# A depthwise convolution of 31 taps as three filters of half the taps, in a kernel ordered by a planner

## The chip, the cores and the metric

The kernel runs on one core of a Trainium2 chip. The metric is device time of one launch in microseconds (us). Before the change the median of three runs is 1378.37 us (1372.61 to 1379.06).

The engines are named as in the profile: PE (TensorE, matmuls; PEld its weight loads), DVE (VectorE), ACT (ScalarE), POOL (GpSimd) and SP (SyncE, which here only issues transfers). SBUF is the memory on the core, PSUM the small memory that PE writes its results to.

## The reference

One inference step of a streaming encoder of two layers, on 512 frames of a new stream ("prompt") and 64 frames of a running one ("sample"), with 1024 channels, all in fp32. A layer, cut to what matters:

```python
p = x @ w_in                                  # [q | k | v | conv_a | conv_gate]
q, k, v, ca, cg = split(p)
attn = differential_attention(rope(q), rope(k), v)      # 4 heads, two softmaxes each
u = ca * sigmoid(cg)                          # 512 channels
full = concat([hist, u], axis=1)              # 30 older frames ahead of the new ones
c = conv(full, conv_w) + conv_b               # each channel by itself, causal, 31 taps
c = silu(layer_norm(c))
y = concat([attn, c]) @ w_out
x = layer_norm(DEEPNORM_ALPHA * x + y)
h = square(relu(x @ w_ff1))                   # 4096 wide
x = layer_norm(DEEPNORM_ALPHA * x + h @ w_ff2)
```

The outputs are x of both streams, and the new keys, values and last 30 convolution inputs of each layer.

## The kernel before

**Data.** x is kept transposed: eight tiles of 128 channels by 576 frames, 512 of the prompt and 64 of the sample. Most work is done in two halves of 288 frames. `r` tiles hold the running fp32 values, `x` and `a` tiles the split operands of matmuls.

**Matmuls.** An fp32 product is made of three matmuls of a reduced fp32 type (`tri`, L734 to L736): high part of the weight by high part of x, high by low, low by high. A weight unit is 128 x 1024. It is loaded into `raw` by SP's queue, and ACT makes the high part `wh` (L891). The low part `wl` is made in one of two ways. Either DVE or POOL subtracts the high part from `raw` (L894). Or, "by transfer": ACT writes minus the high part into `wl` (L875), POOL issues a transfer that adds the weight from memory into it (L878), and ACT writes `wh` (L881). A number `DM` for each stage says what share of the units goes by transfer. While layer 0's FFN runs, 20 weight units of layer 1 are split in advance and stored (`split_ahead`). The FFN's products are taken in pairs with shared sums and differences (L2162, L2030, L1884, L2056, L2273).

**Stages of a layer.** Mixing (input projection, attention, convolution), then the output projection with the first LayerNorm, the FFN, and the FFN's last part with the second LayerNorm. In the attention, the softmax of a block of queries runs over DVE (the maximum, L1486; reciprocals, L1517; the difference of the two softmaxes, L1530) and ACT (the exponential, L1502), and PE transposes the result (L1539). L1615 and L1625 scale its output.

**The convolution** (`conv`, L1305). The 512 channels are four tiles. For each, `ub` holds 30 older frames, 512 of the prompt, 30 older, and 64 of the sample: 636 in a row, and the 606 results (UC) include 30 that nobody needs. `NPTS[t]` of the 31 taps are made by ACT (a product, L1322) and POOL (a sum, L1325), 9 to 12 a tile, into an `r` tile. The others are made by DVE, one instruction a tap (L1337: frames times the tap plus what is there), accumulating in a PSUM tile `sc` read as 2 x 303. Three sums (`fin`, L1344) add the two. Behind it, the channels are added up over tiles (L1669), PE makes the mean (L1679), a reciprocal root is found by a short chain of DVE steps on 96 x 6 values (`rstd`, L959 to L987), and the result is split into high and low parts for the output projection (L1761 and the line behind it).

**The LayerNorms.** The attention's and the convolution's parts of the output projection come in turn. The first is added to alpha x in two steps (L1799, and L1804 for the other summand), the second by L1857. The channel tiles are summed (L1835) and PE makes the mean from that; L1052 subtracts it, L1058 and L1064 square and add up, L1133 multiplies by the reciprocal root, L1141 scales and shifts on ACT, and L1154 makes the low part.

**What sets the order.** Each step is a node with a cost for each engine that may do it (`cV`, `cA`, `cG`, `cP`, `cD` for DVE, ACT, POOL, PE and the load queue), a latency, buffers that it takes and gives back, and a priority. `Sched.run` goes through time with these costs and gives each engine, when it is free in the plan, the ready node of highest priority. In that order the instructions are then issued: nothing is reordered on the chip, an engine runs its rows one after the other. Eight tables of numbers (`PHASES`, one for each of four stages in each layer) set priorities, the share by transfer, the order of weight units and who takes which step. The semaphore waits between instructions follow from which tiles they read and write.

## Time and profile before

| | |
|---|---|
| median of three runs | 1378.37 us (1372.61, 1379.06, 1378.37) |
| the profiled execution's own time | 1375.67 us |
| its span, first to last instruction | 1373.9 us, 24858 instructions |
| mean granted clock of TensorE | 0.977 |
| PE, DVE, ACT, POOL busy | 1308.0, 1078.1, 705.1, 302.3 us |
| transfers | 186.38 MB, mean 136 GB/s |

The stages stand at about 18 to 290 us (mixing and first LayerNorm of layer 0), 290 to 671 (its FFN), 671 to 700 (second LayerNorm), 700 to 965, 965 to 1349 and from 1349 (the same of layer 1). Busy times are sums over the whole span; a stage's own limit is read from its own window. A chain of waits is followed back from the last instruction, and names for each stretch the engine that was then being waited for.

### The profile page before, as it was taken

What the parts mean: (1) busy time and instruction counts of PE and PEld (TensorE: products, weight loads), DVE (VectorE), ACT (ScalarE), POOL (GpSimd) and SP (SyncE); (2) the same over time, 40 slices, a digit from 0 to 9 for tenths busy, and PEclk for the clock granted to TensorE, in tenths of its full rate; (3) what the DMA queues carried; (4) which work ended last, traced back from release to release, by engine and by line L of the source; (5) the groups of instructions that cost most, each with busy time, mean ns of one, the idle gap of its engine ahead of it and who ended that gap; (6) DMA issues with size and microseconds to landing.
All of it is one profiled execution on the core that took longest, in us unless ns stands there. A gap on an engine that the chain in (4) does not pass through costs nothing.

```text
span 1373.9 us, 24858 instructions
## 1 busy us (share of the span) xinstructions
PE 1308.0 (95%) x9518; PEld 1264.1 (92%) x9518; DVE 1078.1 (78%) x2206; ACT 705.1 (51%) x1413; POOL 302.3 (22%) x292
## 2 busy tenths in 40 slices
PE   8989989979999999999999999899989999999997
PEld 7878879979899999999998988798889999999996
DVE  5899998777888887878658999868677676767737
ACT  5766677265444444434156657754654443434424
POOL 0456620150000000000144885223400000000013
PEclk9999989989999999999999999899999999999998
DMA  6635533334465645554345444454234343435262
GB/s 220 162 94 140 122 117 106 93 130 156 144 211 165 208 168 192 185 167 139 102 158 204 160 152 121 129 135 118 64 79 117 112 108 108 124 80 144 70 152 69
DMA packets 70102, 186.38 MB, mean 136 GB/s; under 512 B 10848, under 2 KB 16608, under 8 KB 69984
## 3 DMA queue, kind: packets, MB, share of 16 engines
q1 hardware_dynamic: 63504, 161.20, 34.9%
q0 software_dynamic: 6480, 23.60, 10.4%
q8 instruction: 75, 1.23, 0.4%
q14 instruction: 43, 0.35, 0.1%
HBM read 154.11 MB, written 30.65 MB: 134 GB/s over the span
## 4 chain that ended last, share of the span: by engine, by line
PE 72%; DVE 18%; issue 3%; DMA 2%; ACT 2%; POOL 2%; SPq 0%; ACTq 0%; DVEq 0%; POOLq 0%
PE b L734 21%; PE b L735 21%; PE b L736 21%; DVE sc L1337 8%; DMA raw<-in_wu_dram 2%; PE sc L734 1%; PE b L1006 1%; POOL sq L1064 1%; PE sc L736 1%; PE b L1568 1%; PE sc L735 1%; DVE nm L1486 1%; DVE P L1530 1%; DMA wl<-in_wu_dram 1%; PE b L1611 1%
## 5 line engine op out<-in xcount | busy, mean ns | idle before, releaser
L734 PE MATMUL b<-x,wh 128*128 128x288 f32 x1356 | 416.2, 307 | 6.6 <-ACT wh L891 4.0
L736 PE MATMUL b<-x,wl 128*128 128x288 f32 x1356 | 406.1, 299 | 7.0 <-DVE wl L894 4.8
L735 PE MATMUL b<-x,wh 128*128 128x288 f32 x1356 | 406.5, 300 | 1.7 <-DVE x L1215 1.1
L734 PE MATMUL b<-a,wh 128*128 128x288 f32 x1088 | 325.0, 299 | 0.2 <-ACT x L731 0.2
L735 PE MATMUL b<-a,wh 128*128 128x288 f32 x1088 | 321.3, 295 | 0.0
L736 PE MATMUL b<-a,wl 128*128 128x288 f32 x1088 | 321.0, 295 | 0.0
L734 PEld LDWEIGHTS b<-x,wh 128*128 128x128 f32 x1356 | 260.5, 192 | 13.5 <-ACT wh L891 4.0
L736 PEld LDWEIGHTS b<-x,wl 128*128 128x128 f32 x1356 | 260.2, 192 | 8.2 <-DVE wl L894 5.3
L735 PEld LDWEIGHTS b<-x,wh 128*128 128x128 f32 x1356 | 260.6, 192 | 4.0 <-DVE x L1215 2.5
L734 PEld LDWEIGHTS b<-a,wh 128*128 128x128 f32 x1088 | 205.1, 188 | 2.0 <-issue 0.6
L735 PEld LDWEIGHTS b<-a,wh 128*128 128x128 f32 x1088 | 205.4, 189 | 0.5
L736 PEld LDWEIGHTS b<-a,wl 128*128 128x128 f32 x1088 | 205.1, 188 | 0.0
L2273 DVE TENSOR_TENSOR r<-r,b 128x288 f32<-128x288 f32 x192 | 85.7, 450 | 87.6 <-PE b L736 87.3
L1337 DVE SCALAR_TENSOR_TENSOR sc<-ub,par,sc 128x606 f32<-128x606 f32 x160 | 136.2, 851 | 4.2
L878 POOL DMA_DIRECT2D wl<-in_wu_dram x45 | 39.2, 871 | 446.8 <-ACT wl L875 387.6
L1064 POOL TENSOR_TENSOR sq<-sq,sq 128x288 f32<-128x288 f32 x40 | 35.7, 910 | 416.1 <-ACT sq L1058 415.5
L1325 POOL TENSOR_TENSOR r<-r,prod 128x606 f32<-128x606 f32 x72 | 113.7, 1580 | 54.8 <-ACT prod L1322 31.0
L891 ACT CAST wh<-raw 128x1024 fp32r<-128x1024 f32 (+1 forms) x73 | 71.4, 979 | 71.2 <-PE b L735 52.3
L2056 ACT CAST wh<-ckv 128x512 fp32r<-128x512 f32 x104 | 64.1, 620 | 76.7 <-PE b L735 61.2
L894 DVE TENSOR_TENSOR wl<-raw,wh 128x1024 fp32r<-128x1024 f32 (+1 forms) x73 | 84.5, 1161 | 22.3 <-ACT wh L891 21.7
L1884 DVE TENSOR_TENSOR wl<-ckv,wh 128x512 fp32r<-128x512 f32 x104 | 71.1, 685 | 6.0 <-ACT wh L2056 5.8
L875 ACT ACTIVATE wl<-raw 128x1024 fp32r<-128x1024 f32 x45 | 47.7, 1060 | 44.2 <-PE b L736 25.5
(320 smaller groups left out, 2409.9 us busy)
## 6 DMA issues: line engine op xcount, KB each, us to landing
raw<-in_wu_dram SPq DMA_DIRECT2D x110, 512.0 KB, 4.6
wl<-in_wu_dram POOLq DMA_DIRECT2D x45, 512.0 KB, 7.2
wscr<-cs SPq DMA_DIRECT2D x80, 256.0 KB, 2.0
ckv<-in_wu_dram SPq DMA_DIRECT2D x26, 512.0 KB, 3.6
ah<-in_wu_dram SPq DMA_DIRECT2D x26, 512.0 KB, 4.4
cs<-in_wu_dram SPq DMA_DIRECT2D x40, 256.0 KB, 2.8
wh<-wscr SPq DMA_DIRECT2D x20, 512.0 KB, 3.3
wl<-wscr SPq DMA_DIRECT2D x20, 512.0 KB, 4.4
```

The source lines that it names most:

```text
L734: TE.matmul(o, wh, xh, start=start, stop=False)
L735: TE.matmul(o, wh, xl, start=False, stop=False)
L736: TE.matmul(o, wl, xh, start=False, stop=stop)
L875: S.activation(wt["lo"], wt["raw"], AF.Copy, scale=-1.0)
L891: S.copy(wt["hi"][:, c], wt["raw"][:, c])
L894: e.tensor_tensor(wt["lo"][:, c], wt["raw"][:, c], wt["hi"][:, c].bitcast(F32), op=ALU.subtract)
L1064: e.tensor_tensor(q[a]["t"], q[a]["t"], q[b]["t"], op=ALU.add)
L1325: GP.tensor_tensor(cc[t], cc[t], st[j], op=ALU.add)
L1337: V.scalar_tensor_tensor(st["a0"], win(j), w, st["a0"], op0=ALU.mult, op1=ALU.add)
L1884: e.tensor_tensor(o, a, b, op=ALU.subtract)
L2056: S.copy(tl["wh"][box["i"]][:, off:off + n], src())
L2273: V.tensor_tensor(rr, rr, bk(), op=ALU.add)
```

## The change

**The convolution in three filters.** Call the even frames e, the odd ones o, and the 31 taps' even and odd numbered ones w0 and w1 (16 and 15). One kind of output needs w0 on e plus w1 on o, the other w0 on o plus w1 on e. The change makes three filters of half the frames: a = w0 on e (16 taps), b = w1 on o (15 taps, with the bias), and c = the sums of neighbouring taps on s = e + o (16 taps). The second kind of output is then c minus a minus b. So 47 taps of 303 frames take the place of 31 taps of 606. e and o are read from `ub` with a step of two frames; s lies unit by unit.

- b is made on ACT and POOL (304 frames wide, the first `NPTS[t]` taps, at most 15), and any further taps by DVE.
- s is one sum on DVE or POOL (318 frames).
- a (L1414) and c (L1421) are made on DVE by turns, a tap of one, then a tap of the other. Both accumulate in one PSUM tile `sc`, a in its first half, c in its second.
- `fin` has six instructions (256 and 32 frames, for a + b, c - b, and that minus a). The result lies with its even frames first, and is put back in turn where it is split into high and low parts (`halves`).
- `params` makes the summed taps `cv` once a layer.

```diff
         def conv(t, start, outs):
-            npt = NPTS[t]
+            npt = min(NPTS[t], W // 2)
...
+            def frames(odd, i, n):
+                return ub[t].rearrange("p (n two) -> p two n", two=2)[:, odd, i:i + n]
...
-                a = op({"A": cA(UC, 1 if j else 2)}, pa, (*start, pd), acq=("r",) if j == 0 else ("prod",), pri=PT)
+                a = op({"A": 0.46 if j else 0.5}, pa, (*start, pd), acq=("r",) if j == 0 else ("prod",), pri=PT)
...
+            def both(e):
+                e.tensor_tensor(cc[t][:, :UH], frames(0, 0, UH), frames(1, 0, UH), op=ALU.add)
+            sm = op({"V": cV(UH), "G": cG(UH)}, both, (*start, cc["n", t]), pri=PT)
             vt = None
-            for j in range(npt, W):
+            for j in range(W // 2 + 1):
                 def va(e, j=j):
...
-                        V.scalar_tensor_tensor(st["a0"], win(j), w, st["a0"], op0=ALU.mult, op1=ALU.add)
-                vt = op({"V": cV(UC, True) + 0.06}, va, (*start, pd, vt), acq=("cv", "sc") if j == npt else (), pri=PT)
+                    if j == 0:
+                        st["s"] = take("sc")
+                        st["a"], st["c"] = st["s"][:, 0, :YH], st["s"][:, 1, :YH]
...
+                        V.scalar_tensor_tensor(st["a"], frames(0, j, YH), w, st["a"], op0=ALU.mult, op1=ALU.add)
+                def vc(e, j=j):
...
+                        V.scalar_tensor_tensor(st["c"], cc[t][:, j:j + YH], w, st["c"], op0=ALU.mult, op1=ALU.add)
+                vt = a_end = op({"V": 0.45}, va, (*start, pd, vt), acq=("cv", "sc") if j == 0 else (), pri=PT)
+                vt = op({"V": 0.45}, vc, (sm, vt, ld_n), pri=PT)
...
             def fin(e):
-                for o, i, b, c, n in ((0, 0, 0, 0, hc), (hc, hc, 1, 0, SEQ - hc), (SEQ, S0, 1, S0 - hc, DEC)):
-                    V.tensor_tensor(a1[:, o:o + n], a1[:, i:i + n], a0[:, b, c:c + n], op=ALU.add)
+                parts = ((0, 0, SEQ // 2), (SEQ // 2, S0 // 2, DEC // 2))
+                for o, i, n in parts:
+                    V.tensor_tensor(cc[t][:, o:o + n], st["a"][:, i:i + n], b_(n, i), op=ALU.add)
+                for o, i, n in parts:
+                    V.scalar_tensor_tensor(cc[t][:, T // 2 + o:T // 2 + o + n], st["c"][:, i:i + n], cv[:, t, 0:1],
+                                           b_(n, i + 1), op0=ALU.add, op1=ALU.subtract)
+                for o, i, n in parts:
+                    z = cc[t][:, T // 2 + o:T // 2 + o + n]
+                    V.tensor_tensor(z, z, st["a"][:, i:i + n], op=ALU.subtract)
```

**The plan.** A low part by transfer had a fixed latency of 6.5 us in the plan. Now it has 1.9 + 2.93, plus what the load queue is still busy with, and 2.93 us are booked on that queue. Costs are changed too: a tap of a or c 0.45 us, `fin` 1.4 for 0.9, a step of the reciprocal root 0.16 for 0.075 and the root as one node 1.75 for 1.6, a load of x 200 for 144 columns, and the extra 0.1 (`PD`) that a PE node waited for another engine's result is gone. A filler matmul (`keep`, `spare`) is added with its share `FT` at 0, so that none is issued. All eight tables of `PHASES` are written anew.

```diff
-PD = 0.1
-DM, GD, GDL = 0.0, 0.88, 6.5
+PD = 0.0
+DM, GD, GDL, GDS = 0.0, 0.88, 1.9, 2.93
...
+                        if n.dm:
+                            n.lat = GDL + n.dm + max(0.0, busy["D"] - t - c)
+                            busy["D"] = max(busy["D"], t + c) + n.dm
...
-                los.append(op({"G": GD}, acc, (m,), lat=GDL, pri=pri + 1000, two=False))
+                los.append(op({"G": GD}, acc, (m,), lat=GDL + GDS, pri=pri + 1000, two=False))
+                los[-1].dm = GDS
...
-            m = op({"V": 0.075}, s, (m,), pri=pri, two=True)
+            m = op({"V": 0.16}, s, (m,), pri=pri, two=True)
...
-  'NPT': '9,10,12,12',
+  'NPT': '14,16,16,13',
```

**How the order moves.** In a row, the line comes first, then the operation, the tile written and those read with the numbers of their buffers, the shape, and the semaphores waited for: one for each engine or transfer queue whose work must have come so far.

DVE, layer 0, the first taps of the first channel tile, before (L1335, L1337), between rows of the attention's softmax:

```order
L1335 TENSOR_SCALAR sc_119<-ub_544,par_161 128x2x303 [waits DMAHW3_49,Pool_49]
L1517 RECIPROCAL rc_598<-sums_592 128x2 [waits Activation_49]
L1518 TENSOR_TENSOR rc_598<-rc_598,nlam_162 128x1 [waits DVE_49]
L1337 SCALAR_TENSOR_TENSOR sc_119<-ub_544,par_161,sc_119 128x2x303
L1337 SCALAR_TENSOR_TENSOR sc_119<-ub_544,par_161,sc_119 128x2x303 [waits DVE_49]
L1485 MEMSET sc_118 64x2x64 [waits PE_49]
L1486 TENSOR_REDUCE nm_596<-sc_118 128x2 [waits DVE_49]
L1337 SCALAR_TENSOR_TENSOR sc_119<-ub_544,par_161,sc_119 128x2x303
L1530 SCALAR_TENSOR_TENSOR P_603<-P_603,rc_598 128x128 [waits Activation_49]
L1337 SCALAR_TENSOR_TENSOR sc_119<-ub_544,par_161,sc_119 128x2x303 [waits DVE_49] x3
```

A tap waits for DVE's own count when the row ahead of it is the tap that it adds to.

DVE, layer 0, after the change, the first taps of the second tile (L1412 and L1414 are filter a, L1419 and L1421 filter c):

```order
L1412 TENSOR_SCALAR sc_118<-ub_881,par_161 128x303 [waits DMAHW4_49,DVE_49,Pool_49]
L1580 TENSOR_REDUCE nm_962<-sc_119 64x2
L1582 TENSOR_REDUCE nm_962<-b_114 64x1
L1582 TENSOR_REDUCE nm_962<-b_115 64x1
L1583 TENSOR_TENSOR nm_581<-nm_962 64x2 [waits DVE_49]
L1419 TENSOR_SCALAR sc_118<-r_93,par_161 128x303 [waits Pool_49]
L1414 SCALAR_TENSOR_TENSOR sc_118<-ub_881,par_161,sc_118 128x303 [waits DVE_49]
L1421 SCALAR_TENSOR_TENSOR sc_118<-r_93,cv_165,sc_118 128x303 [waits DVE_49]
```

The taps now come in pairs, one of each filter.

DVE, layer 0, a little later in the same tile, where rows of other work stand between two taps:

```order
L1036 SCALAR_TENSOR_TENSOR ary_1211<-art_1213,ary_1211 96x6
L1039 SCALAR_TENSOR_TENSOR ary_1211<-arh_1215,ary_1211 96x6 [waits DVE_49]
L1048 SCALAR_TENSOR_TENSOR dg_1237<-ident,ary_1211 96x576 [waits DMAHW7_49,DVE_49]
L1414 SCALAR_TENSOR_TENSOR sc_118<-ub_881,par_161,sc_118 128x303
L1421 SCALAR_TENSOR_TENSOR sc_118<-r_93,cv_165,sc_118 128x303 [waits DVE_49]
L1414 SCALAR_TENSOR_TENSOR sc_118<-ub_881,par_161,sc_118 128x303 [waits DVE_49]
L1706 SCALAR_TENSOR_TENSOR ob_853<-ob_853,gs_163,b_114 128x288 [waits PE_49,Activation_49]
```

The first tap behind other rows has no wait; those right behind a tap of the other filter have one, though they read and write the other half of the tile.

PE, layer 1, around the mean of the convolution's LayerNorm (L1679), before, with score matmuls of the attention ahead of it and the first matmuls of the next product behind:

```order
L736 MATMUL sc_118<-ckh_8234,a_8037 128x512
L734 MATMUL b_116<-a_8527,a_8036 128x64
L735 MATMUL b_116<-a_8528,a_8036 128x64
L736 MATMUL b_116<-a_8527,a_8037 128x64
L1679 MATMUL sc_119<-sgm_101,ones_h 128x288 [waits DVE_49]
L1679 MATMUL sc_119<-sgm_101,ones_h 128x288
L734 MATMUL b_115<-x_7307,wh_83 128x288 [waits DMAHW1_49]
```

Here the mean is the first thing behind the scores.

PE at the same place after the change (L1770; L781 to L783 are the three matmuls of `tri`, L1630 is the softmax's transpose):

```order
L783 MATMUL b_117<-x_7468,wl_87 128x288
L781 MATMUL b_117<-x_7472,wh_83 128x288
L782 MATMUL b_117<-x_7473,wh_83 128x288
L783 MATMUL b_117<-x_7472,wl_87 128x288
L1770 MATMUL sc_119<-sgm_101,ones_h 128x288 [waits DVE_49,Activation_49]
L1770 MATMUL sc_119<-sgm_101,ones_h 128x288
L1630 MATMUL b_115<-ident,P_9267 128x128 [waits DVE_49]
```

The mean now stands behind matmuls of a projection, 990 rows behind the end of layer 0's last LayerNorm where it was 925; in layer 0 it is PE's row 985 where it was 1017.

DVE, layer 0, before, where the output projection's second part is added (L1857) and the tiles are summed for the first LayerNorm's mean (L1835):

```order
L1835 TENSOR_TENSOR sg_107<-sg_107,r_98 128x288 [waits DVE_49]
L1857 TENSOR_TENSOR r_94<-r_94,b_116 128x288 [waits PE_49]
L1835 TENSOR_TENSOR sg_107<-sg_107,r_94 128x288 [waits DVE_49]
L1857 TENSOR_TENSOR r_92<-r_92,b_115 128x288 [waits PE_49]
L1835 TENSOR_TENSOR sg_107<-sg_107,r_92 128x288 [waits DVE_49]
L1857 TENSOR_TENSOR r_93<-r_93,b_114 128x288 [waits PE_49]
L1835 TENSOR_TENSOR sg_107<-sg_107,r_93 128x288 [waits DVE_49]
```

Each sum follows the addition that it needs, on the same engine.

POOL, after the change, the same sums (L1927), with the residual additions (L1896, before L1804) ahead of them:

```order
L1896 TENSOR_TENSOR r_98<-r_98,x_2467 128x288 [waits DMAHW6_49,DVE_49]
L1896 TENSOR_TENSOR r_94<-r_94,x_2492 128x288 [waits DMAHW7_49,DVE_49]
L1927 TENSOR_TENSOR sg_107<-r_97,r_91 128x288 [waits DVE_49]
L1927 TENSOR_TENSOR sg_107<-sg_107,r_95 128x288 [waits DVE_49,Pool_49]
L1927 TENSOR_TENSOR sg_107<-sg_107,r_92 128x288 [waits DVE_49,Pool_49]
L1927 TENSOR_TENSOR sg_107<-sg_107,r_96 128x288 [waits DVE_49,Pool_49]
L1927 TENSOR_TENSOR sg_107<-sg_107,r_93 128x288 [waits DVE_49,Pool_49]
```

The sums for this mean, a chain in which each waits for the one ahead, have moved from DVE to POOL, and so have the additions.

More of the change, by code (lines that the diff above doesn't have):

```diff
@@ L563, in delay, with spare, left_p @@
         return 0.2 if "P" in (a, b) else 0.13
+    def spare(self, t, busy, avail):
+        if not FT or self.keep is None or busy > t + 1e-9 or not self.free["b"] or not self.left_p():
+            return False
+        return sum(min(b, t) - max(a, t - FW) for a, b in self.recent if b > t - FW) < FT * FW
+    def left_p(self):
+        while self.plast and self.plast[-1].at is not None and self.plast[-1] in self.done:
+            self.plast.pop()
+        return bool(self.plast)
     def run(self, engines):
@@ L648, in run @@
             assert times, ("stuck", count, len(self.nodes), self.free, [(n.acq, n.fn) for n in avail[:10]])
+            if self.spare(t, busy["P"], avail):
+                n = self.op({"P": FC}, lambda e: self.keep(e, self.free["b"][0]))
+                n.left, n.at, self.now = 0, t, {}
+                busy["P"] = t + FC
+                self.recent = [x for x in self.recent if x[1] > t - FW] + [(t, t + FC)]
+                a = t
+                while a < t + FC - 1e-9:
+                    k = int(a / HAMW + 1e-9)
+                    b = min(t + FC, (k + 1) * HAMW)
+                    act[k] = act.get(k, 0.0) + b - a
+                    a = b
+                n.fn(engines["P"])
+                count += 1
+                continue
             t = min(times)
@@ L736, in tri, with keep @@
         TE.matmul(o, wl, xh, start=False, stop=stop)
+    def keep(e, k):
+        TE.matmul(tl["b"][k][:, :128], ones_d, ones_d, start=True, stop=True)
+    sch.keep = keep
     def bank():
```

716 lines of the change are left out of this document (373 added, 343 removed).

## The prediction

> **What bounds the kernel now.** I read the page's first and fourth parts, then a table of windows by stage, a second one cut at the convolution, PE's waits, and the rows of the operations that the change touches.
>
> ```profile
> span 1373.9 us, 24858 instructions
> PE 1308.0 (95%) x9518; PEld 1264.1 (92%) x9518; DVE 1078.1 (78%) x2206; ACT 705.1 (51%) x1413; POOL 302.3 (22%) x292
> PE 72%; DVE 18%; issue 3%; DMA 2%; ACT 2%; POOL 2%; SPq 0%; ACTq 0%; DVEq 0%; POOLq 0%
> ```
>
> PE is busy 95% of the span, yet 18% of the chain that ended last is DVE. Where that is, the windows show (columns: window, its length, busy time and count of PE, PE's weight loads, DVE, ACT and POOL, granted clock, DMA share, GB/s).
>
> ```profile
> 18.00:290.00 272.00, 246.15 (x1723) 229.72 (x1722) 236.74 (x465) 175.60 (x372) 112.73 (x97) 0.94 0.46 123
> 290.00:671.00 381.00, 376.04 (x2801) 374.16 (x2802) 306.41 (x610) 165.53 (x305) 8.51 (x11) 0.99 0.50 167
> 700.00:965.00 265.00, 250.42 (x1778) 232.61 (x1776) 220.48 (x443) 160.72 (x356) 128.16 (x112) 0.97 0.49 145
> 965.00:1349.00 384.00, 378.73 (x2839) 376.06 (x2839) 268.16 (x560) 168.16 (x303) 30.61 (x36) 1.00 0.39 104
> ```
>
> Rows 2 and 4 are the two FFNs: PE is idle for 5.0 and 5.3 us at a clock of 0.99 and 1.00. There the matmuls are the time, and the change keeps them, so less DVE or ACT work in them is worth only a part of those few us. Rows 1 and 3 are the mixing stages: idle 25.9 and 14.6 us, and the clock of 0.94 costs layer 0 another 16 us at most (6% of 272). So about 65 us are open to a change of this kind, nearly all in the mixing stages. These I cut at the first convolution tap on DVE, the last of its closing sums, and the end of the first LayerNorm:
>
> ```profile
> 46.00:159.00 113.00, 102.26 (x723) 97.67 (x723) 107.33 (x160) 78.45 (x149) 74.61 (x57) 0.95 0.47 113
> 732.00:836.50 104.50, 100.58 (x744) 95.84 (x743) 101.33 (x159) 68.14 (x144) 80.88 (x61) 1.00 0.44 148
> 159.00:291.00 132.00, 119.74 (x822) 109.07 (x822) 112.57 (x271) 83.38 (x195) 35.82 (x37) 0.92 0.40 117
> 836.50:967.00 130.50, 120.98 (x835) 109.23 (x835) 104.67 (x251) 79.12 (x178) 42.91 (x45) 0.95 0.49 123
> ```
>
> While the taps run (rows 1 and 2, layers 0 and 1) DVE is busy 95% and 97%: it sets when the convolution ends. Behind it (rows 3 and 4) it is at 85% and 80%, and PE loses 12.3 and 9.5 us idle, plus up to 11 and 7 us to the clock. PE's waits name the owners:
>
> ```profile
> PE sc L734 <- DVE r L2271: 7.1, 12, 0.6
> PE b L736 <- DVE wl L894: 4.8, 1, 4.8
> PE b L1541 <- DVE P L1530: 4.4, 1, 4.4
> PE b L1539 <- DVE P L1530: 4.3, 3, 1.9
> PE sc L734 <- DVE r L1344: 3.2, 1, 3.2
> PE b L736 <- DMA wl<-in_wu_dram: 1.9, 2, 1.2
> ```
>
> The columns are us in total, times, and the longest. DVE is the releaser of five of these six; the single 4.8 us for a weight's low part is where layer 0's FFN begins, as the timeline shows:
>
> ```profile
> 284.97 0.61 PE L736 MATMUL b<-x,wl 128*128 128x288 f32 x1 [4.83 <-DVE wl L894]
> ```
>
> **The convolution on DVE.** Before, 168 taps of 606 elements, 87 in layer 0 and 81 in layer 1. After, 256 of 303 (the filters a and c), 8 more taps of the filter b, 3 sums, and six closing rows a tile for three. The prices:
>
> ```profile
> L1337 DVE SCALAR_TENSOR_TENSOR sc<-ub,par,sc 128x606 f32<-128x606 f32 x160 | 136.2, 851 | 4.2
> 762.37 17.75 DVE L1337 SCALAR_TENSOR_TENSOR sc<-ub,par,sc 128x606 f32<-128x606 f32 x20
> 279.91 1.91 DVE L1052 TENSOR_TENSOR r<-r,b 128x288 f32<-128x288 f32 x5
> L2273 DVE TENSOR_TENSOR r<-r,b 128x288 f32<-128x288 f32 x192 | 85.7, 450 | 87.6 <-PE b L736 87.3
> L1884 DVE TENSOR_TENSOR wl<-ckv,wh 128x512 fp32r<-128x512 f32 x104 | 71.1, 685 | 6.0 <-ACT wh L2056 5.8
> 781.09 0.87 DVE L1344 TENSOR_TENSOR r<-r,sc 128x303 f32<-128x303 f32 x3
> ```
>
> Twenty taps in a row, each adding to what the last one wrote, take 17.75 us: (17.75 - 0.851) / 19 = 0.889 us from start to start, more than one lasts. Five rows that don't depend on each other take 1.91: (1.91 - 0.450) / 4 = 0.365, less than one lasts. An element costs (685 - 450) / 224 = 1.05 ns. So a tap of 303 comes every 0.889 - 303 x 1.05 ns = 0.571 us if it waits for the row ahead of it, and every 0.365 + 15 x 1.05 ns = 0.381 if not; a tap of 606 without that wait, by the same step, 0.699. Which holds is seen in the change's order: a and c are halves of one PSUM tile, and every tap carries a wait for DVE's own count when the row ahead is the other filter's, though it does not read its result; only a tap behind some other row has none. I take 0.571, the waiting price, for the 174 of 256 taps that stand right behind another one, and 0.381 for the other 82; before, 116 of 168 waited: 174 x 0.571 + 82 x 0.381 = 130.6 against 116 x 0.889 + 52 x 0.699 = 139.5, so -8.9 us over both layers, -7 in layer 0 and -2 in layer 1. If the turns did hide the wait it would be 256 x 0.381 = 97.5, -42. That is the lower end; the upper is all of them waiting, 146.2, +7.
>
> The Trainium skill ("VectorE: DVE Perf Modes", The DRAIN you can't avoid) says that the next DVE operation starts only when the pipe is empty, that semaphores between them add nothing, and that the number of operations is to be kept low: a rule against splitting 168 into 256. This trace disagrees with its first half, since rows of 450 ns start every 365, and by its rule the waits above would be free. The same page's formula for fp32 sums, (N + 151) / 0.96 ns, gives an estimate of 473 ns for 303 elements and 789 for 606: 256 x 0.473 - 168 x 0.789 = -11.5 us, near the -8.9 of the rows, and no end of the range.
>
> Closing rows: three take 0.87 now. Six are three of 256 elements, 0.33 each unwaited by the price above, and three of 32, 0.1 to 0.2 each; I take 1.5, so +2.6 a layer (range +1 to +4). Eight taps of b and three sums at 0.45 each: +3 in layer 0, +2 in layer 1. The rest is what the new order puts between first tap and last closing row: in layer 0 other DVE rows grow from 62 to 71 (three low parts of weights leave, ten small softmax rows and moves come in), in layer 1 from 62 to 87 (a second sample softmax, a second reciprocal root chain, a low part). By their rows' durations these are about +5 and +14. DVE's work in the tap window so goes from 107.3 to about 112 in layer 0 (+4) and from 101.3 to about 118 in layer 1 (+17).
>
> **ACT and POOL.** ACT's taps go from 80 of 606 to 112 of 304, POOL's sums from 72 of 606 to 104 of 304.
>
> ```profile
> L1325 POOL TENSOR_TENSOR r<-r,prod 128x606 f32<-128x606 f32 x72 | 113.7, 1580 | 54.8 <-ACT prod L1322 31.0
> L1154 POOL TENSOR_TENSOR x<-r,x 128x288 fp32r<-128x288 f32 x48 | 39.9, 852 | 43.1 <-ACT x L731 41.4 <-DVE r L1052 1.2
> L1322 ACT ACTIVATE prod<-ub,par 128x606 f32<-128x606 f32 x72 | 56.7, 801 | 11.9 <-POOL r L1325 11.5
> L1058 ACT ACTIVATE sq<-r 128x288 f32<-128x288 f32 x64 | 25.4, 440 | 60.9 <-DVE r L1052 59.6 <-POOL sq L1064 0.9 <-PE b L736 0.4
> ```
>
> POOL: 104 x 0.86 = 89 for 113.7; ACT: 112 x 0.45 to 0.55 = 50 to 62 for 64. In the tap windows POOL is 66 and 77% busy, ACT 69 and 65%, and DVE ends last, so this is worth nothing; were DVE relieved, POOL's shorter chain would keep up.
>
> **Behind the convolution.** Fifteen residual additions (L1804) and 18 sums for a LayerNorm's mean (L1835) go from DVE to POOL.
>
> ```profile
> L1804 DVE TENSOR_TENSOR r<-r,x 128x288 f32<-128x288 f32 x32 | 15.6, 491 | 0.9
> ```
>
> 15 x 0.49 + 18 x 0.45 = 15.5, nearly all in layer 0, where DVE falls from 112.6 to about 97 (-16) before the first LayerNorm's end; in layer 1 it falls from 105 to 104. As DVE is 85% busy there, I take 0.85 of the 16 as time: -13. At 0.852 a row POOL gets 28 us more beside its 36 of 132, and holds them; but its seven sums for one mean stand in a chain, and the last, for which PE waits, lasts 0.4 longer than on DVE: a part of what the range's upper end stands for.
>
> **PE's work is moved too.** In the order, the convolution's mean on PE comes 32 PE rows earlier in layer 0, and 65 later in layer 1 (counted from the last LayerNorm). A matmul in a saturated stretch costs 50 us / 380 = 0.132:
>
> ```profile
> 500.00:550.00 50.00, 50.00 (x380) 50.00 (x379) 42.65 (x85) 22.54 (x38) 0.00 (x0) 1.00 0.56 186
> ```
>
> So 4 us of matmuls lie behind instead of ahead of layer 0's convolution, and 9 ahead instead of behind in layer 1.
>
> **Weights' transfers.** 15 more low parts are made by POOL's adding transfers (60 for 45) and 15 fewer by DVE: 24 in layer 0, against 9 the other way in layer 1.
>
> ```profile
> L894 DVE TENSOR_TENSOR wl<-raw,wh 128x1024 fp32r<-128x1024 f32 x65 | 81.2, 1251 | 21.3 <-ACT wh L891 20.9
> L878 POOL DMA_DIRECT2D wl<-in_wu_dram x45 | 39.2, 871 | 446.8 <-ACT wl L875 387.6
> wl<-in_wu_dram POOLq DMA_DIRECT2D x45, 512.0 KB, 7.2
> L875 ACT ACTIVATE wl<-raw 128x1024 fp32r<-128x1024 f32 x45 | 47.7, 1060 | 44.2 <-PE b L736 25.5
> ```
>
> In layer 0, 24 x 1.25 = 30 us leave DVE, 24 x 0.87 = 21 come to POOL and 24 x 1.06 = 25 to ACT, with 12 MB for the queues; in layer 1, 11 us come back to DVE. Those in the FFNs lie under a saturated PE; those in the mixing stages are in the counts of rows above and below. What counts is the FFN's start: there every second first unit now comes by transfer, so the 4.8 us wait for DVE is about halved, while the 7.2 us of a landing cost something if asked late: -2 (range -5 to +4). Booking these transfers on the load queue only moves when loads are issued; SP's queue has room for it (DMA share 0.50 in that FFN), so nothing.
>
> **The end.** Two of ACT's last eight scalings go to POOL, 4.25 / 8 = 0.53 us each, so -1 at most, and nothing if POOL is the later:
>
> ```profile
> 1366.09 4.25 ACT L1141 ACTIVATE r<-r,par 128x288 f32<-128x288 f32 x8 [1.62 <-DVE r L1133]
> ```
>
> **Costed at nothing.** The filler matmul (its share FT is 0, none is issued); the plan's new costs for taps, root chain and x loads, which issue no instruction and act only through the order counted above; the four copies and four subtractions a layer that now read two halves and write every second element (576 elements as before, on engines with room behind the convolution); the summed taps, two short rows a layer before any tap is due.
>
> **Sum.** Layer 0: +4 in the tap window, +4 of matmuls carried over, -13 behind: -5 (range -13, the moved matmuls and taps costing nothing, to +4, the relief worth little because the LayerNorm's chain waits, not DVE's load). Layer 1: DVE at 97% stretches the window by 17, 9 of it is filled with matmuls that the next one no longer has, -2 behind: +6 (range -5, the taps at their unwaited price, to +12). FFN -2, end -1. In all -2, against the profiled execution's own 1375.67 us (span 1373.9 and 1.8 around it): 1373.7. The median of the runs is 1378.37, 0.2% above that execution; I leave the forecast at 1374.
>
> **Rivals.**
> *The relief pays (faster).* Layer 0 reaches its -13, layer 1 comes out level as the added rows fill gaps of DVE that the taps' waits leave (174 waits of up to 0.19 us, 33 us in all), the FFN -2: 1375.7 - 15 = about 1360. For it: five of the six waits above end on DVE; against it: in layer 1 nothing leaves DVE.
> *Layer 1's convolution ends late (slower).* If the 9 us of matmuls moved ahead are not waiting to be done when DVE runs late, the 17 stand whole, and layer 0 gives nothing: 1375.7 + 17 - 2 = 1391. It decides if that window, 104.5 now, is over 115. For it: 97% DVE, and softmax rows that PE waits for (L1530) queue behind taps.
> *Every second frame is read slowly.* Filters a and b read in steps of 8 bytes, which no row here does. Were such a read two elements' time, the 136 taps of a and b would cost 303 x 1.05 ns more each, 43 us: up to 1410. No run here shows what the Trainium skill states ("SBUF — State Buffer", on cachelines): 16-byte lines, full bandwidth from two hits in a line, which such a step still has.
> *The turns hide the wait after all.* Then DVE is 33 us lighter than I sum, and with two thirds of that on the path it is 1374 - 22, about 1352. The order's waits speak against it.
>
> **How the numbers follow.** Chances: forecast 0.42 (own range 1366 to 1384), relief pays 0.28, late convolution 0.22, slow reads 0.05, hidden wait 0.03. Half a per cent, 6.9 us, is about what a measurement tells from no change: below 1371.5 is faster, above 1385.3 slower. Faster: 0.26 + 0.03 + 0.12 of the forecast = 0.41; same: 0.27 + 0.02 + 0.02 = 0.31; slower: 0.20 + 0.05 + 0.03 = 0.28. The range 1357 to 1390 takes in the relief and most of the late convolution.
>
> **What would show it.** In the changed kernel's profile: the PSUM taps of a and c at starts 0.57 apart where they follow each other (0.38: the turns hide); the tap window of layer 1 near 120 us with DVE above 95%, of layer 0 near 117; the stretch behind layer 0's at 122 or less; the sums of POOL near 0.85; no PE wait over 5 us for a landing low part; FFNs still at 381 and 384. A tap of a that lasts as long as now, or a wait for transfers of tens of us, would prove the sum wrong.

## The result and the profile after

The change takes 1392.91 us (median of 4 runs, 1389.63 to 1396.17), against 1376.71 for the kernel before on the same chip: a ratio of 1.0125, 95% interval 1.0098 to 1.0153. It is slower by 16 us, and outside the predicted range by 3. The profiled execution took 1390.61 us.

The page of the changed kernel, its span, engines, and chain of waits by engine and by line:

```profile
span 1388.8 us, 25260 instructions
PE 1312.2 (94%) x9548; PEld 1264.2 (91%) x9548; DVE 1078.6 (78%) x2344; ACT 693.4 (50%) x1396; POOL 299.4 (22%) x366
PE 51%; DVE 19%; DMA 16%; ACT 4%; issue 3%; POOL 1%; SPq 0%; ACTq 0%; DVEq 0%; POOLq 0%
PE b L781 15%; PE b L783 14%; PE b L782 14%; DMA wscr<-cs 6%; DMA cs<-in_wu_dram 6%; DVE sc L1414 3%; DVE sc L1421 3%; DMA wl<-in_wu_dram 2%; DVE cs L879 1%; PE sc L781 1%; PE b L1067 1%; DMA ah<-in_wu_dram 1%; ACT cs L875 1%; PE sc L783 1%
```

DVE is as busy as before to half a microsecond (1078.1 there), so the filters and what left DVE for POOL took nothing off it in sum. New in the chain are 16% of DMA, which had 2%. Twelve of them are the loads and stores of the weights that layer 0's FFN splits ahead for layer 1 (`cs`, `wscr`); the adding transfers themselves are 2%.

To see where the time went I cut both executions where PE has done the same matmuls. The two kernels have 9374 matmuls in common. Beside these they have some that add up squares for the LayerNorms, and here the change has 30 more (144 before, 174 after; count, then shortest, median and longest in ns):

```profile
L1006 PE MATMUL b<-ones_c,sq x132: 165/223/320, 270.2 to 1361.7; 128*96 128x1 f32 x132
L1006 PE MATMUL sc<-ones_c,sq x12: 223/223/244, 964.0 to 964.9; 128*96 128x1 f32 x12
L1067 PE MATMUL b<-ones_c,sq x150: 164/223/244, 262.0 to 1375.4; 128*96 128x1 f32 x150
L1067 PE MATMUL sc<-ones_c,sq x24: 164/223/223, 970.8 to 972.7; 128*96 128x1 f32 x24
```

The kernel before (window, length, busy time and count of PE, PEld, DVE, ACT, POOL, granted clock, DMA share, GB/s):

```profile
0.00:390.00 390.00, 353.98 (x2463) 333.89 (x2464) 325.29 (x648) 236.13 (x496) 122.10 (x118) 0.95 0.48 138
390.00:661.40 271.40, 271.40 (x2050) 271.40 (x2049) 220.77 (x435) 114.59 (x201) 0.00 (x0) 1.00 0.52 173
661.40:700.10 38.70, 37.95 (x290) 37.06 (x289) 26.10 (x68) 13.35 (x33) 13.61 (x17) 0.99 0.35 124
700.10:965.20 265.10, 250.52 (x1777) 232.71 (x1777) 220.44 (x443) 160.72 (x356) 128.37 (x112) 0.97 0.49 145
965.20:1329.50 364.30, 359.09 (x2695) 356.99 (x2695) 256.44 (x533) 163.45 (x294) 25.30 (x30) 1.00 0.40 108
1329.50:1373.90 44.40, 35.09 (x251) 32.05 (x249) 29.09 (x82) 16.85 (x35) 12.96 (x16) 0.90 0.23 66
```

and the change:

```profile
0.00:381.80 381.80, 349.24 (x2476) 328.18 (x2477) 315.42 (x683) 245.95 (x525) 135.05 (x169) 0.98 0.56 153
381.80:662.30 280.50, 275.66 (x2050) 272.32 (x2049) 206.07 (x423) 122.40 (x211) 10.37 (x12) 1.00 0.65 195
662.30:700.30 38.00, 37.92 (x290) 36.81 (x289) 24.98 (x70) 15.07 (x35) 14.51 (x18) 0.99 0.43 139
700.30:973.90 273.60, 251.20 (x1789) 233.78 (x1789) 232.82 (x521) 154.98 (x362) 99.68 (x118) 0.97 0.41 131
973.90:1341.20 367.30, 361.21 (x2696) 359.14 (x2696) 273.44 (x578) 140.48 (x235) 19.85 (x23) 1.00 0.38 103
1341.20:1388.80 47.60, 37.00 (x256) 33.99 (x255) 25.83 (x74) 14.53 (x31) 19.97 (x26) 0.86 0.15 50
```

Row by row: layer 0's mixing stage with the start of its FFN is 8.2 us shorter, and the main part of that FFN 9.1 longer. The next row is 0.7 shorter. Layer 1's mixing stage is 8.5 longer, its FFN 3.0, the end 3.2. The sum is 14.9, the difference of the two spans. Of the 30 added matmuls 12 stand in the first row, 12 in the fourth and 6 in the last. They are 6.6 us of PE's time in all; what they cost the kernel is not shown, since PE has idle time in these rows.

The second row is the surprise. PE was busy through all of it before; now 4.8 us are idle, and the same 2050 matmuls keep PE busy 4.3 us longer too. DVE has less to do there (206 for 221 us). What rose is the DMA share, from 0.52 to 0.65: 12 adding transfers are issued in this stretch, where the kernel before issues none. PE's waits in that stretch, for which the kernel before had no row at all (us in total, times, longest):

```profile
PE b L781 <- DVE sgm L2254: 1.4, 2, 0.9
PE b L783 <- DMA wl<-in_wu_dram: 1.3, 2, 0.8
PE b L783 <- DVE wl L1976: 1.2, 2, 1.0
PE b L781 <- DVE r L2365: 0.9, 3, 0.4
```

No wait is long; they are many small ones with different releasers. The DMA issues of this stretch (count, KB each, median us to landing), in the kernel before

```profile
raw<-in_wu_dram SPq DMA_DIRECT2D x25, 512.0 KB, 3.9
```

and in the change

```profile
raw<-in_wu_dram SPq DMA_DIRECT2D x25, 512.0 KB, 6.7
wl<-in_wu_dram POOLq DMA_DIRECT2D x12, 512.0 KB, 8.2
```

show that the plain loads of weights land 2.8 us later beside the adding transfers.

The convolution's operations, grouped, and six rows of the timeline in layer 1 (start, duration; rows between 780.62 and 784.19 are left out):

```profile
L1414 DVE SCALAR_TENSOR_TENSOR sc<-ub,par,sc 128x303 f32<-128x303 f32 x120 | 64.4, 536 | 3.3
L1421 DVE SCALAR_TENSOR_TENSOR sc<-r,cv,sc 128x303 f32<-128x303 f32 x120 | 64.3, 536 | 3.1
```

```profile
779.47 0.54 DVE L1421 SCALAR_TENSOR_TENSOR sc<-r,cv,sc 128x303 f32<-128x303 f32 x1
780.04 0.54 DVE L1414 SCALAR_TENSOR_TENSOR sc<-ub,par,sc 128x303 f32<-128x303 f32 x1
780.62 0.54 DVE L1421 SCALAR_TENSOR_TENSOR sc<-r,cv,sc 128x303 f32<-128x303 f32 x1
784.19 0.52 DVE L1430 TENSOR_TENSOR r<-sc,r 128x256 f32<-128x256 f32 x2
784.65 0.77 DVE L1432 SCALAR_TENSOR_TENSOR r<-sc,cv,r 128x256 f32<-128x256 f32 x2
785.34 0.51 DVE L1436 TENSOR_TENSOR r<-r,sc 128x256 f32<-128x256 f32 x2
```

A tap behind the other filter's tap comes 0.57 us after it: over the 167 such pairs of the execution the mean is 0.572. Filter a's taps, which read every second frame, last exactly as long as c's, which read unit by unit. The six closing rows take 1.66 us (784.19 to 785.85). The stretches from the first tap to the last closing row, layer 1 and layer 0:

```profile
731.00:850.00 119.00, 110.94 (x805) 103.65 (x805) 112.66 (x249) 73.51 (x179) 63.64 (x77) 0.99 0.41 136
41.00:161.50 120.50, 110.16 (x764) 103.70 (x763) 112.51 (x235) 88.50 (x184) 64.40 (x81) 0.94 0.60 140
```

DVE is busy for 95% and 93% of them, so it still sets their length. By the rows themselves, from the start of the first tap to the end of the last closing row, they are 118.2 us (731.9 to 850.1) and 119.5 (41.9 to 161.4), for 104.8 (731.8 to 836.6) and 114.7 (45.9 to 160.6) before: 13.4 and 4.8 us more.

### The profile page after: what moved, and what is told of

The parts are those of the page before. It is cut to its first block, busy times and chain, and to the rows that moved or that the text cites. A ratio compares the mean times of both kernels' runs of the same rounds, so it can differ in the third digit from the quotient of the medians.

```text
span 1388.8 us, 25260 instructions
## 1 busy us (share of the span) xinstructions
PE 1312.2 (94%) x9548; PEld 1264.2 (91%) x9548; DVE 1078.6 (78%) x2344; ACT 693.4 (50%) x1396; POOL 299.4 (22%) x366
## 4 chain that ended last, share of the span: by engine, by line
PE 51%; DVE 19%; DMA 16%; ACT 4%; issue 3%; POOL 1%; SPq 0%; ACTq 0%; DVEq 0%; POOLq 0%
PE b L781 15%; PE b L783 14%; PE b L782 14%; DMA wscr<-cs 6%; DMA cs<-in_wu_dram 6%; DVE sc L1414 3%; DVE sc L1421 3%; DMA wl<-in_wu_dram 2%; DVE cs L879 1%; PE sc L781 1%; PE b L1067 1%; DMA ah<-in_wu_dram 1%; ACT cs L875 1%; PE sc L783 1%; PE sc L782 1%
## 5 line engine op out<-in xcount | busy, mean ns | idle before, releaser
L781 PE MATMUL b<-x,wh 128*128 128x288 f32 x1356 | 415.9, 307 | 12.8 <-ACT wh L952 5.1
L783 PE MATMUL b<-x,wl 128*128 128x288 f32 x1356 | 404.8, 298 | 5.3 <-DVE wl L955 2.8
L781 PE MATMUL b<-a,wh 128*128 128x288 f32 x1088 | 326.3, 300 | 6.4 <-ACT x L778 3.3
L783 PE MATMUL b<-a,wl 128*128 128x288 f32 x1088 | 321.7, 296 | 1.6 <-DMA wl<-in_wu_dram 1.6
L781 PEld LDWEIGHTS b<-x,wh 128*128 128x128 f32 x1356 | 259.2, 191 | 21.4 <-ACT wh L952 4.4
L783 PEld LDWEIGHTS b<-x,wl 128*128 128x128 f32 x1356 | 259.2, 191 | 6.7 <-DVE wl L955 3.1
L781 PEld LDWEIGHTS b<-a,wh 128*128 128x128 f32 x1088 | 205.0, 188 | 10.5 <-ACT x L778 3.6
L938 POOL DMA_DIRECT2D wl<-in_wu_dram x60 | 52.2, 871 | 745.7 <-ACT wl L935 378.8
L783 PEld LDWEIGHTS b<-a,wl 128*128 128x128 f32 x1088 | 205.4, 189 | 2.3 <-DMA wl<-in_wu_dram 2.3
L952 ACT CAST wh<-raw 128x1024 fp32r<-128x1024 f32 (+1 forms) x58 | 55.6, 960 | 72.6 <-PE b L782 54.0
L1392 POOL TENSOR_TENSOR r<-r,prod 128x304 f32<-128x304 f32 x104 | 79.6, 765 | 47.3 <-ACT prod L1389 21.9
L935 ACT ACTIVATE wl<-raw 128x1024 fp32r<-128x1024 f32 x60 | 63.5, 1058 | 37.9 <-PE b L783 33.3
L955 DVE TENSOR_TENSOR wl<-raw,wh 128x1024 fp32r<-128x1024 f32 (+1 forms) x58 | 65.6, 1132 | 18.4 <-ACT wh L952 18.1
L879 DVE TENSOR_TENSOR cs<-cs 128x512 fp32r<-128x512 f32 x40 | 31.0, 776 | 49.3 <-ACT cs L875 49.1
L875 ACT CAST cs<-cs 128x512 fp32r<-128x512 f32 x40 | 24.8, 620 | 85.3 <-DMA cs<-in_wu_dram 84.8
```

The lines of the kernel that those rows point to most:

```text
L781: TE.matmul(o, wh, xh, start=start, stop=False)
L783: TE.matmul(o, wl, xh, start=False, stop=stop)
L879: e.tensor_tensor(b["t"][:, :D // 2], b["t"][:, :D // 2].bitcast(F32), b["t"][:, D // 2:D].bitcast(F32), op=ALU.subtract)
L935: S.activation(wt["lo"], wt["raw"], AF.Copy, scale=-1.0)
L938: GP.dma_start(wt["lo"], wu[l, i], accum_op=ALU.add)
L952: S.copy(wt["hi"][:, c], wt["raw"][:, c])
```

## The experiments

The theory after the result: two places lose the time, layer 1's convolution, because the taps wait on each other through the shared tile, and layer 0's FFN, because of transfers. All runs below are told with their ratio to the kernel before, in runs on the same chip. Where an edit leaves the plan alone, the order of all instructions is the changed kernel's; where it doesn't, the planner orders everything anew, and the tables were not fitted to that.

### Filter c in a tile of its own, in SBUF

```diff
+    cacc = sb_p.tile([128, YH + 1], F32, name="cacc")
...
-                        st["a"], st["c"] = st["s"][:, 0, :YH], st["s"][:, 1, :YH]
+                        st["a"], st["c"] = st["s"][:, 0, :YH], cacc[:, :YH]
```

> The changed kernel with filter c accumulating in a tile of its own in SBUF instead of in the second half of a's PSUM tile; the order of all instructions is unchanged. Theory (the taps wait on each other through the shared tile, and layer 1's convolution ends 13 us late by it): pairs of taps come 0.38 to 0.45 us apart instead of 0.571, some 167 x 0.15 = 25 us leave DVE, layer 1's last closing sum comes 8 to 12 us earlier against the same start, and the kernel takes 1375 to 1384 us, 8 to 15 less than the change. Rival (the loss is in the order of PE's work and in layer 0's FFN): taps faster, but the end moves by less than 3 us, 1389 to 1393.

1394.42 us, ratio 1.0148 (1.0126 to 1.017): nothing won. The theory's time was wrong, but not for the rival's reason, as the groups show (a is L1415, c L1422):

```profile
L1422 DVE SCALAR_TENSOR_TENSOR cacc<-r,cv,cacc 128x303 f32<-128x303 f32 x120 | 80.5, 671 | 0.2
L1415 DVE SCALAR_TENSOR_TENSOR sc<-ub,par,sc 128x303 f32<-128x303 f32 x120 | 63.3, 528 | 0.2
```

The wait for the row directly ahead is gone, and c follows a by 0.44 us. But c's taps now last 671 ns on average. DVE's timeline at one place, and POOL's:

```profile
801.28 0.53 DVE L1415 SCALAR_TENSOR_TENSOR sc<-ub,par,sc 128x303 f32<-128x303 f32 x1
801.72 1.26 DVE L1422 SCALAR_TENSOR_TENSOR cacc<-r,cv,cacc 128x303 f32<-128x303 f32 x1
```

```profile
800.98 1.67 POOL L1477 TENSOR_TENSOR a<-r,a 128x576 fp32r<-128x576 f32 x1
```

The tap of 1.26 us stands beside a POOL subtraction of 1.67 us, and ends 0.33 us behind it. Sorted by that, the 90 c taps that overlap a POOL operation last 718 ns, the 30 others 527; a's taps, which add to PSUM, last 526 and 530. So an operation of DVE with both inputs in SBUF is held up by POOL's, and one with its second input in PSUM is not. The Trainium skill ("SBUF — State Buffer", Who interferes with whom) states this for two SBUF inputs; these numbers agree.

### The same, without POOL's sums

```diff
                 def ga(e, j=j):
+                    return
                     GP.tensor_tensor(b_(), b_(), st[j], op=ALU.add)
```

> Filter c accumulating in SBUF as in the first experiment, and POOL's sums of filter b left out (b is then its first tap alone), so that POOL reads and writes nothing beside the taps; the order of all else is unchanged. Theory (in the first experiment c's taps in SBUF lasted 718 ns beside POOL's sums and 527 without them, which ate what the missing wait gave): every c tap lasts 520 to 560 ns, pairs come 0.44 to 0.48 us apart, layer 1's last closing sum comes 7 to 11 us earlier against the same start than in the changed kernel, and the kernel takes 1379 to 1386. Rival (something other than POOL stretches them, or nothing behind the convolution follows it): taps of c above 600 ns on average, or an end within 3 us of 1393.

1374.55 us, ratio 0.9996 (0.9973 to 1.0019): 18 us less than the change, more than was expected. (The two profiled executions differ by 11.)

```profile
L1423 DVE SCALAR_TENSOR_TENSOR cacc<-r,cv,cacc 128x303 f32<-128x303 f32 x120 | 73.5, 613 | 0.2
L1416 DVE SCALAR_TENSOR_TENSOR sc<-ub,par,sc 128x303 f32<-128x303 f32 x120 | 63.6, 530 | 0.2
```

c's mean of 613 ns is what the expectation gave to the rival: 24 of the 120 taps stand beside POOL's other work and last 958; the other 96 last 526, and a follows a c tap by 0.445 in the median. The stretches of the taps, layer 1 and layer 0:

```profile
726.00:834.20 108.20, 105.90 (x784) 99.36 (x782) 106.12 (x244) 69.06 (x171) 27.20 (x24) 1.00 0.43 144
44.00:152.00 108.00, 102.22 (x744) 97.09 (x743) 103.67 (x230) 84.43 (x180) 26.17 (x28) 0.98 0.65 155
```

They end at 834 and 152 us instead of 850 and 161, PE's order being the same; from the first tap on they are 7.9 and 9.8 us shorter (110.3 and 109.7). So what holds up the taps costs a large part of what the change loses. That all of it is the taps' distance is not shown, because the edit also takes POOL's chain of b away. No closing row had waited for that chain: in both stretches of the changed kernel no wait of DVE names POOL. But DVE's other rows there are 1.7 us shorter in sum in layer 1 and 3.9 in layer 0 without POOL's sums beside them, and the main part of layer 0's FFN, with the same transfers, is 3.1 shorter (277.4 for 280.5), which is not explained.

### Half of layer 1's taps on DVE

```diff
                 def va(e, j=j):
+                    if l == 1 and j >= 8:
+                        return
```

and the same in `vc`.

> The changed kernel with the second half of filter a's and c's taps left out in layer 1 (64 of its 128 taps on DVE issue nothing, so the convolution is incomplete); the order of all else is unchanged. Theory (DVE's work sets the end of layer 1's convolution): 64 x 0.54 = 35 us leave DVE, the last closing sum comes at least 10 us earlier against the same start, the first LayerNorm 7 us or more, kernel 1380 to 1386. Rival (PE's order or the attention sets it): the LayerNorm's end moves by under 3 us.

1380.86 us, ratio 1.0045 (1.0021 to 1.0068), as the theory said. The first LayerNorm has its mean subtracted 7.3 us earlier (960.7 for 968.0), as it said too.

```profile
733.00:840.00 107.00, 105.25 (x783) 99.25 (x782) 80.49 (x180) 70.87 (x171) 64.29 (x77) 1.00 0.44 145
```

30 us of DVE's busy time are gone (1048.4 in all for 1078.6) and DVE is idle for a quarter of the stretch, which is only 9 us shorter, where at least 10 was expected (from the second tap to the last closing row 733.7 to 839.9, for 735.0 to 850.1): PE is now the one at 98%. So DVE's excess there was about 9 us, and below that the matmuls that the new order puts ahead of the convolution's mean set the length.

### A quarter of the columns by transfer in layer 0's FFN

```diff
+                    q = D // 4 if l == 0 and i >= 28 else D
-                    GP.dma_start(wt["lo"], wu[l, i], accum_op=ALU.add)
+                    GP.dma_start(wt["lo"][:, :q], wu[l, i][:, :q], accum_op=ALU.add)
```

> The changed kernel with the 19 adding transfers of layer 0's FFN moving only the first quarter of the columns (the other three quarters of those low parts are left as minus the weight); the order is unchanged. Theory (layer 0's FFN loses 9 us because the queues are 64% busy with these transfers, so that weights come late): the stretch from 380 to 662 us shortens by 6 to 9 us, kernel 1383 to 1387. Rival (the order of DVE's rows in that FFN loses it, or the weights split ahead): under 2 us gained.

1387.46 us, ratio 1.0101 (1.0068 to 1.0134), just above the theory's 1383 to 1387. The stretch in question, cut at the same matmuls, its loads, and the chain of waits of the whole kernel:

```profile
382.90:654.80 271.90, 271.90 (x2050) 271.90 (x2049) 207.92 (x422) 124.04 (x210) 10.34 (x12) 1.00 0.57 184
raw<-in_wu_dram SPq DMA_DIRECT2D x25, 512.0 KB, 4.9
PE 71%; DVE 18%; ACT 2%; DMA 2%; issue 2%; POOL 0%; DVEq 0%; SPq 0%; ACTq 0%; POOLq 0%
```

271.9 us for 280.5 (271.4 before), PE without a gap again, at the same order of every engine and with the same instructions: only the bytes of 19 transfers are fewer. The stretch doesn't vary by so much from one execution to the next: in the other four runs here that keep the changed order up to there it takes 277.4 to 280.6. So the loss in that FFN, 8.6 of 9.1 us, is the traffic. Whether PE misses the low parts that the adding transfers bring, or the loads beside them, the run doesn't tell apart.

The kernel's median follows less: it is 13.4 us above that of the kernel before on its chip, for 16.2, and the two ratios' intervals overlap. In the profiled execution 7.6 us are still there at layer 1's first taps (727.4 for 735.0), 3.9 at the last row of its output projection (958.0 for 961.9), 2.9 at the end. They go in layer 1's mixing stage:

```profile
692.50:972.00 279.50, 256.84 (x1791) 239.62 (x1790) 233.39 (x524) 155.01 (x362) 99.58 (x118) 0.95 0.41 128
```

The same work keeps PE busy 5.6 us longer here than in the changed kernel's execution, at a granted clock of 0.95 for 0.97, and the stage is 5.9 longer. In the run of the last stage, below, the clock there is 0.95 too, and the stage takes 277.3 us. So what is lost again there goes with the clock of that execution; the edit touches nothing in layer 1.

### No transfers in that FFN

```diff
-  'DM': 0.5,
+  'DM': 0,
```

in the table of layer 0's FFN; the order is planned anew.

> The change with the share by transfer set to 0 in layer 0's FFN as before (43 adding transfers for 60); planned anew. Theory (these transfers cost that FFN 9 us): its main part back to 270 to 274 us, kernel 1380 to 1387. Rival (DVE can't take 17 more low parts in that stage): FFN unchanged or longer, 1390 or more.

1389.27 us, ratio 1.0135 (1.0082 to 1.0187), above the theory's 1380 to 1387.

```profile
0.00:387.80 387.80, 354.18 (x2475) 334.03 (x2476) 318.97 (x687) 240.81 (x522) 134.95 (x164) 0.96 0.53 146
387.80:660.20 272.40, 272.06 (x2050) 271.83 (x2049) 216.65 (x429) 116.89 (x205) 0.87 (x1) 1.00 0.54 175
```

The main part is at 272 us as the theory said, but the same matmuls ahead of it end at 388 instead of 382. 8.1 us are won and 6 lost, and the total can't be told from the change's own. What the new order loses at the FFN's start was not tried further.

### One part of the change at a time

The convolution of before under the new plan, with its own shares of taps:

```diff
-            npt = min(NPTS[t], W // 2)
+            npt = NPTS[t]
...
-                vt = a_end = op({"V": 0.45}, va, (*start, pd, vt), acq=("cv", "sc") if j == 0 else (), pri=PT)
-                vt = op({"V": 0.45}, vc, (sm, vt, ld_n), pri=PT)
+                vt = op({"V": cV(UC, True) + 0.06}, va, (*start, pd, vt), acq=("cv", "sc") if j == npt else (), pri=PT)
...
-  'NPT': '14,16,16,13',
+  'NPT': '9,10,12,12',
```

> The change with the convolution of before (31 taps of 606, its own costs and shares of taps), but the new plan: tables, booked transfers, costs. Theory (the convolution itself is about even, the plan's tables lose in layer 0's FFN): 1388 to 1400 with layer 0's FFN again about 9 us longer than before. Rival (the three filters lose the time): 1372 to 1380.

1420.97 us, ratio 1.0314 (1.0266 to 1.0362), far above what either theory said. Layer 0's FFN has the change's loss here too: its main part takes 279.3 us.

The three filters under the plan of before (tables, costs and transfers undone, the new `NPT` kept):

```diff
-PD = 0.0
-DM, GD, GDL, GDS = 0.0, 0.88, 1.9, 2.93
+PD = 0.1
+DM, GD, GDL, GDS = 0.0, 0.88, 6.5, 0.0
...
-            m = op({"V": 0.16}, s, (m,), pri=pri, two=True)
+            m = op({"V": 0.075}, s, (m,), pri=pri, two=True)
```

> The change's convolution, with its shares of taps for ACT and POOL, under the plan of before: its tables, transfers at a fixed 6.5 us, its costs. Theory: layer 0's FFN back to 271 us for its main part, taps at 0.571, layer 1's convolution near 838 to 845; 1373 to 1385. Rival (the filters lose the time whatever the plan): 1388 or more.

1383.46 us, ratio 1.0073 (1.0046 to 1.01), as the theory said. The taps come 0.572 us apart, and layer 1's last closing row ends at 840.6; the main part of layer 0's FFN takes 274.1 us, where 271 was expected. In layer 0 its FFN's rows end 1.3 us earlier than before (660.1 for 661.4), and layer 1's first LayerNorm has its mean subtracted 7.7 us later (967.9 for 960.2): the loss is in layer 1 under this plan too. A part of it may be the clock, 0.95 in that stage for 0.97.

The plan of before, with the filters in layer 0 alone (`conv_old` is the function before):

```diff
-                conv(t, (m, h, z), (o1, o2))
+                (conv if l == 0 else conv_old)(t, (m, h, z), (o1, o2))
```

> The plan of before, with the three filters in layer 0 alone and layer 1's convolution as before. Theory (in layer 1 the filters cost about 8 us, in layer 0 they bring 1 to 3): 1369 to 1377, level with or a little under the kernel before. Rival (the filters cost in either layer): 1380 or more.

1372.44 us, ratio 0.9991 (0.9972 to 1.001): level, as the theory said. Set against the run ahead of it, the filters in layer 1 cost 0.8%, 11 us, under this plan.

The new tables without the booking on the load queue:

```diff
-DM, GD, GDL, GDS = 0.0, 0.88, 1.9, 2.93
+DM, GD, GDL, GDS = 0.0, 0.88, 6.5, 0.0
```

> The change with its transfers at a fixed 6.5 us in the plan again, and nothing booked on the load queue; the tables stay, so the order is planned anew. Theory (booking was not what costs; the transfers themselves are): layer 0's FFN still 6 to 10 us longer than before, kernel 1385 to 1405. Rival (booking delays loads): 1375 to 1384.

1407.24 us, ratio 1.0244 (1.0211 to 1.0277), above the theory's range. The main part of layer 0's FFN takes 280.1 us, so its loss doesn't come from the booking. Here and in the first of these four the tables meet a plan that they weren't made for, and the times are 14 and 28 us above the change's. I read this as the misfit, since both parts by themselves can't bring so much; that is argued, not shown, and neither run tells the price of the part that was undone.

### The last stage

The last table (the FFN's last part and the second LayerNorm of layer 1) as before, which leaves the order alone up to there:

```diff
-  'DM': 0,
+  'DM': 1,
...
-  'RP': [1, 7],
+  'RP': [],
```

> The change with the last of its eight tables (layer 1's last part of the FFN and its second LayerNorm) as before; the order of all engines is the same up to that stage. Theory (the new table's sums and scalings on POOL cost the end 2 to 3 us): the stretch from the last matmul of the FFN's main part to the end of the span is 44 to 45 us instead of 47.6, kernel 1389 to 1391. Rival (it is the clock there, not the order): 46 us or more.

1391.67 us, ratio 1.0102 (1.0062 to 1.0142), not to be told from the change. The stretch from the same row to the end of the span:

```profile
1346.20:1391.40 45.20, 35.08 (x251) 32.23 (x249) 28.87 (x82) 16.88 (x35) 12.85 (x16) 0.86 0.23 64
```

45.2 us for 47.6, between the theory's 44 to 45 and the rival's 46. In the four other runs that keep the changed order to the end, the same stretch takes 46.3 to 47.0, and this run has six of the added sums of squares on PE fewer. So 1 to 2 us of the end's 3.2 seem to be its order; with medians this close it stays open.

### Two PSUM tiles, and plans fitted to the costs

```diff
-                        st["s"] = take("sc")
-                        st["a"], st["c"] = st["s"][:, 0, :YH], st["s"][:, 1, :YH]
+                        st["a"], st["c"] = take("b")[:, :YH], take("b")[:, :YH]
...
-                vt = a_end = op({"V": 0.45}, va, (*start, pd, vt), acq=("cv", "sc") if j == 0 else (), pri=PT)
+                vt = a_end = op({"V": 0.43}, va, (*start, pd, vt), acq=("cv", "b", "b") if j == 0 else (), pri=PT)
```

The plan's other costs and its transfers are those of before, and the tables are moved from those of before until the plan was shorter.

> The three filters with a and c in two PSUM tiles of their own (two of the four single banks in place of a double one), a tap at 0.43 us and the closing rows at 1.6 in the plan, otherwise the costs and transfers of the plan before, and tables moved from those of before until the plan was shorter. Theory (the wait on the shared tile is what makes the filters no better than 31 taps): pairs of taps come 0.44 to 0.46 us apart beside POOL's sums too, no tap above 0.56, kernel 1360 to 1372. Rival (two banks fewer for the projections cost PE what DVE gains): 1373 to 1385.

1358.95 us (1356.54 to 1361.65), ratio 0.9892 (0.9872 to 0.9913): faster than both kernels, and 1 us below the theory's range. Its chain of waits and groups (a is L1403, c L1410):

```profile
PE 75%; DVE 8%; ACT 3%; issue 2%; DMA 1%; POOL 1%; DVEq 0%; SPq 0%; ACTq 0%; POOLq 0%
L1410 DVE SCALAR_TENSOR_TENSOR b<-r,cv,b 128x303 f32<-128x303 f32 x120 | 63.9, 532 | 0.0
L1403 DVE SCALAR_TENSOR_TENSOR b<-ub,par,b 128x303 f32<-128x303 f32 x120 | 63.8, 532 | 0.0
```

The 166 pairs of neighbouring taps come 0.440 us apart, with POOL's sums beside them, and no tap lasts longer than 0.551. Of these rows 158 still carry a wait for DVE's own count; it is now for the row two earlier. The stretches of the taps, layer 1 and layer 0:

```profile
724.00:825.00 101.00, 97.29 (x709) 92.23 (x708) 94.48 (x223) 66.00 (x154) 60.76 (x74) 0.98 0.42 143
47.00:155.00 108.00, 100.65 (x725) 95.73 (x724) 99.28 (x235) 82.05 (x177) 61.46 (x76) 0.97 0.45 114
```

From the first tap, 2 us ahead of these windows, to the end of the last closing row they are 103.2 and 110.0 us, where before they were 104.8 and 114.7, and with the change 118.2 and 119.5. DVE's share of the chain of waits falls from 18% to 8%.

The control is the kernel before with nothing but its tables moved in the same way: numbers, the lists of who takes which step, and in four tables the share by transfer (42 adding transfers for 45). For example:

```diff
-  'PT': 527.0,
+  'PT': 556.34,
```

> The kernel before with nothing but its tables moved in the same way until the plan was shorter: the control for the run beside it. Theory (fitting the tables anew brings something whatever the convolution): 1362 to 1374. Rival (the tables of before can't be bettered by a shorter plan): 1374 to 1385.

1389.76 us, ratio 1.0103 (1.0074 to 1.0133): slower, where 1362 to 1374 was expected. This shorter plan brought nothing by itself; it is one plan, and unlike its neighbour's it was made with the old costs. How much of the 15 us of its neighbour is the second tile and how much its tables was not tried apart.

## Why the prediction was wrong

By its own steps:

- **The taps' price held.** 0.571 us for a tap that waits was worked out from two rows of the kernel before, and 0.572 was measured. That the turns don't hide the wait, read from the waits in the order, was right, and the run with two tiles shows what they would have hidden: 0.440, though not the 0.381 that I took for an unwaited tap. The Trainium skill's rule ("VectorE: DVE Perf Modes", The DRAIN you can't avoid), by which a semaphore costs nothing between two operations (measured there on copies), doesn't hold for a wait on the row directly ahead: 0.13 us a tap hang on which row the wait is for.
- **Reads of every second frame cost nothing**: 536 ns for both filters. That rival is out.
- **Layer 0, -5, and the FFN's start, -2**: together -8.2 was measured. The sign is right and the size near, but the parts are others. The first tap starts 4.0 us earlier, for which the sum had no term. The tap window is 4.8 longer, for +4; the window that the prediction shows for the kernel before ends 1.6 us ahead of its last closing row. What lies behind the taps is 9.0 shorter, for 11.
- **Layer 1, +6**: +8.5, within its range, and that is partly luck. DVE in the tap window was said to reach 118, and has 112.7; the window grew by 13.4 us instead of 17, and what lies behind it shrank by 4.8 instead of 11. The two misses cancel for the most part.
- **The weights' transfers is the step that failed.** Its sentence "Those in the FFNs lie under a saturated PE" counted what DVE, POOL and ACT have to do, and took the room on the queues from one share (0.50). 19 of the transfers fall in that FFN. They take DVE's work off, which was worth nothing there, and beside them the plain loads land later, 6.7 us for 3.9: the main part is 9.1 us longer, 8.6 of which went when the transfers' bytes were cut. So a term set at 0 for the stage was +9, and the range of -5 to +4 spoke of the FFN's start alone.
- **The change was said to keep the matmuls**; it adds 30, 6.6 us of PE's time in LayerNorms. Their price is not known.
- **The end, -1**, was +3.2, and layer 1's FFN, at 0, was +3.0. Neither is explained beyond the 1 to 2 us of the last stage's order.

The rival of the late convolution gave 1391 and so came nearest, and its point of decision (a window over 115) was passed, but its 17 us are not what happened in layer 1, so the nearness is chance: that stage lost 8.5, and the rest came from the FFNs, which no rival named, and from the end.

## What to carry to other kernels

An engine that has no gap in a stage says that less work elsewhere is worth nothing there, not that more traffic is: put the bytes of a step that is moved onto the queues against the loads that the saturated engine waits for, stage by stage. Two chains taken by turns hide each other's latency only if nothing ties them, and a tile that both write ties them; read the wait on each row, and give each chain a tile of its own, in the memory that no other engine holds up. A table fitted to one plan is part of that plan: undoing a cost under it measures the misfit.
